# Low parts of every fourth weight block made by an accumulating DMA, in a two-layer decoder trunk in split fp32

## The chip, the cores and the metric

The kernel runs on one core of one Trainium2 chip. The metric is the device time of one launch in microseconds, the median of three runs. The engines are TensorE (PE, with its weight loads PEld), VectorE (DVE), ScalarE (ACT), GpSimd (POOL) and SyncE (SP, which here only issues DMAs).

## The reference

A decoder trunk with D_MODEL = 2048, 256 tokens, two layers, fp32. Layer 0 uses sliding-window attention with sinks, layer 1 block attention with shared keys and values (with 256 tokens it is causal attention over one block). Each layer also has 4 memory heads into 256 memory tokens, one output projection, a layer norm, an MLP with squared ReLU of width 8192, and a second norm:

```python
mix = concat([self_out, mem_out]) @ w_o[layer]
h = layer_norm(ALPHA * h + mix, ln_g[layer, 0], ln_b[layer, 0])
ffn = square(relu(h @ w_up[layer])) @ w_down[layer]
h = layer_norm(ALPHA * h + ffn, ln_g[layer, 1], ln_b[layer, 1])
```

Nearly all the work is matrix products of 256 tokens with some 350 MB of weights, each weight used once.

## The kernel before

Every operand is kept as an exact pair: a high part rounded to the matrix engine's reduced fp32 format (fp32r), and a low part, the rest. A product is then three products of parts: high by high, high by low, low by high. `split()` (L92) makes a pair: ACT rounds (L93), DVE subtracts the high part from the source (L94).

Weights come in blocks of 128 x 2048 (1 MB). `weights()` (L96) asks for a block with one DMA on SP's queue (L102), into one of 4 raw slots (NRAW), and splits it in two halves of 128 x 1024, each into a high and a low tile; there are 7 slots of each (NHI, three and a half blocks). The raw slot is shared with other 1 MB loads: activations and the gain and bias rows of the layer norm. The first three blocks of the kernel come in parts of 4, 2 and 2 (L398 to L400 in `mem_units`), the others in one.

Three routines consume blocks. `wform()` (L137) takes one block for 128 output columns: 16 k-tiles, each with a 512-column product with the high part (L146) and a 256-column one with the low part (L148). `aform()` (L157) takes four blocks, for 512 output columns: 16 k-tiles, each with three 512-column products for either of two token tiles (L168 to L170); `hold` leaves the second token tile's last products for `finish()`. `mem_units()` (L391) does the same as a generator for the memory tokens (L404 to L406).

A layer runs: values (one aform), then four groups of one key and three query blocks and four memory queries (wform), with the attention heads' stages hooked between the products; the output projection (four aforms); the layer norm `normed()` (L343); the MLP in four chunks of 16 wforms (up) and four aforms (down); the second norm. In layer 0 both norms have a filler: the memory products of layer 1 (mem_v, mem_k: four blocks each). In `normed` the transposes of the normed rows stand after units 10, 11, 12 and 16 of the filler (FILL). In layer 1 the first norm has none, and the aform behind it (`wu1`) holds the whole second token tile. The kernel begins with mem_v and mem_k of layer 0.

The framework draws up the order of each engine's instructions when the kernel is built: by program order, where a planner with its own cost estimates holds an operand ready. At run time each engine goes through its own list in that order and waits at each instruction for its operands and its slot. The inverse standard deviation of a norm (`ln_stat`) runs in small steps on POOL (L309 to L313).

Of the kernel before, what the change touches and what calls it, by code (L numbers as in the profile page):

```python
# [17 lines left out]
T = 256  # L18
# [20 lines left out]


class Stages:
    """The heads in flight; each stage of a head runs inside a later block's matrix products."""

    def __init__(self):
        self.heads = []
# [19 lines left out]
WHOOKS = (10, 14, 4)  # L65
NWARM = 2
FILL = (10, 11, 12, 16)
WTAIL = ((1, 2), (2, 0), (3, 1), (5, 2), (7, 1), (9, 2))


@with_exitstack
def trunk(ctx: ExitStack, tc: tile.TileContext, a: dict, out: bass.AP):
# [6 lines left out]
    ps_mm = ctx.enter_context(tc.tile_pool(name="ps_mm", bufs=4, space=PS))  # L79
    ps_at = ctx.enter_context(tc.tile_pool(name="ps_at", bufs=4, space=PS))  # L80

    # ---------------------------------------------------------------- constants
    ident = const.tile([P, P], F32, name="ident")
    make_identity(nc, ident)
    # the tensor engine's clock comes up while the first blocks are on their way
    warm = ap_.tile([P, 512], F32, name="warm", tag="lg", bufs=NLG)
    nc.vector.memset(warm, 0.0)
    ps_warm = ps_at.tile([P, 512], F32, name="ps_warm", tag="at")
    for i in range(NWARM):
        nc.tensor.matmul(ps_warm, warm[:, :P], warm, start=True, stop=True)  # L90
    # ---------------------------------------------------------------- operand splitting
    def split(hi, lo, src):  # L92
        nc.scalar.copy(hi, src)  # L93
        nc.vector.tensor_tensor(lo, src, hi.bitcast(F32), ALU.subtract)  # L94

    def weights(src, parts=1):  # L96
        """One block of weights on chip as exact (hi, lo) pairs, in two halves; the first block
        of all comes in parts, so that the products can begin early."""
        raw = wp.tile([P, 2048], F32, name="raw", tag="raw", bufs=NRAW)
        n = 2048 // parts  # L100
        for c in range(0, 2048, n):
            nc.sync.dma_start(raw[:, c:c + n], src[:, c:c + n])  # L102
        halves = []
        n = min(n, 1024)
        for s in range(2):
            hi = wp.tile([P, 1024], F32R, name="whi", tag="whi", bufs=NHI)
            lo = wp.tile([P, 1024], F32R, name="wlo", tag="wlo", bufs=NHI)
            for c in range(0, 1024, n):
                split(hi[:, c:c + n], lo[:, c:c + n], raw[:, s * 1024 + c:s * 1024 + c + n])
            halves.append((hi, lo))  # L110
        return halves

# [1 line left out]
        return [ap_.tile([P, 4, 2, T], F32R, name=f"{nm}{j}", tag=f"{tag}{j}") for j in range(KT // 4)]  # L114

    def load_act(src, x, j, parts=1):
        """Four k-tiles of an operand on chip as exact (hi, lo) pairs."""
        raw = wp.tile([P, 4, T], F32, name="raw_x", tag="raw", bufs=NRAW)
        n = 4 // parts
        for k in range(0, 4, n):  # L120
            nc.sync.dma_start(raw[:, k:k + n], src[:, 4 * j + k:4 * j + k + n])
            split(x[:, k:k + n, 0], x[:, k:k + n, 1], raw[:, k:k + n])
# [7 lines left out]
                split(xt[2 * j2 + j][:, :, 0, :], xt[2 * j2 + j][:, :, 1, :], raw[:, j])  # L130
        return xt

    # ---------------------------------------------------------------- matrix products
    def nothing():
        pass

    def wform(src, xt, hooks={}):  # L137
        """PSUM [128 columns of W, 512]: xh.W + xl.W as two halves to be added."""
        halves = weights(src)
        ps = ps_mm.tile([P, 2 * T], F32, name="ps_w", tag="mm")  # L140
        for k in range(KT):
            hooks.get(k, nothing)()
            hi, lo = halves[k // 8]
            kk = (k % 8) * P
            x = xt[k // 4][:, k % 4]
            nc.tensor.matmul(ps, hi[:, kk:kk + P], x.rearrange("p s t -> p (s t)"),  # L146
                             start=(k == 0), stop=False)
            nc.tensor.matmul(ps[:, :T], lo[:, kk:kk + P], x[:, 0], start=False, stop=(k == KT - 1))  # L148
        return ps
# [5 lines left out]
        nc.vector.tensor_tensor(dst, ps[:, :T], sb, ALU.add)  # L155

    def aform(srcs, xts, hold=0, hooks={}):  # L157
        """Two PSUM banks [128 tokens, 512 columns] accumulated over 4 k-tiles per block.

        The second token tile's products with the last `hold` k-tiles wait for finish()."""  # L160
        ps = [ps_mm.tile([P, 512], F32, name="ps_a", tag="mm") for _ in range(NT)]
        n = len(srcs)

        def mms(t, k, hi, lo):
            xh = xts[k // 4][:, k % 4, 0, t * P:(t + 1) * P]
            xl = xts[k // 4][:, k % 4, 1, t * P:(t + 1) * P]
            st, en = k == 0, k == 4 * n - 1
            nc.tensor.matmul(ps[t], xh, hi, start=st, stop=False)  # L168
            nc.tensor.matmul(ps[t], xh, lo, start=False, stop=False)  # L169
            nc.tensor.matmul(ps[t], xl, hi, start=False, stop=en)  # L170

        late = []
        for i, src in enumerate(srcs):
            halves = weights(src)
            for q in range(4):
                hi, lo = halves[q // 2]
                c = slice((q % 2) * 512, (q % 2) * 512 + 512)
                args = (4 * i + q, hi[:, c], lo[:, c])
                hooks.get(4 * i + q, nothing)()
                mms(0, *args)  # L180
                if 4 * i + q >= 4 * n - hold:
                    late.append(args)
                else:
                    mms(1, *args)

        def finish():
            for args in late:
                mms(1, *args)

        return ps, finish  # L190

    # ---------------------------------------------------------------- attention
    def evict_v(ps, nm):
        v = ap_.tile([P, NT, 512], F32, name=nm, tag=nm)
        for t in range(NT):
# [1 line left out]
        return v  # L197

    def evict_mk(ps):
        """K of the memory tokens, transposed to [head dim, head, token]; yields before the transposes."""  # L200
        mk = ap_.tile([P, MH, T], F32, name="mk", tag="mk")
        nat = [ap_.tile([P, 512], F32, name="mk_n", tag="lg", bufs=NLG) for _ in range(NT)]
        for t in range(NT):
            nc.scalar.copy(nat[t], ps[t])
        yield mk
        for t in range(NT):
            pt = ps_at.tile([P, 4, P], F32, name="pt_mk", tag="at")
            for m in range(MH):
                nc.tensor.transpose(pt[:, m], nat[t][:, m * P:(m + 1) * P], ident)
            nc.scalar.copy(mk[:, :, t * P:(t + 1) * P], pt)  # L210
        yield

    def head_out(ot, hd, lg, den, spans, v, vcol):
        """Two more stages: probabilities transposed, then O^T as an exact pair."""
        rec = sm.tile([P, NT], F32, name="rec", tag="rec")
        nc.vector.reciprocal(rec, den)
        for t, (c0, n) in enumerate(spans):
# [2 lines left out]
        pt = ps_at.tile([P, 512], F32, name="pt", tag="at")  # L220
        pts = ap_.tile([P, 512], F32, name="pts", tag="pts", bufs=2)
        full = spans[0][1] == T
        # pt columns: [keys 0..127 x all queries | keys 128..255 x later queries]
        dst = 0
        order = [(0, t) for t in range(NT)] + [(1, t) for t in range(NT) if full or t == 1]
        for s, t in order:
# [55 lines left out]
    def new_q():  # L282
        return ap_.tile([P, T], F32, name="qt", tag="qt", bufs=4)

    # ---------------------------------------------------------------- layer norm
    def ln_rows(li, places):
        """gain and bias, each in parts of (pool, tag, bufs, columns), as four pairs of 512 columns."""
        rows = []
        for src, parts in zip((a["ln_g"], a["ln_b"]), places):
            pieces = []  # L290
            for pool, tag, bufs, n in parts:
                r = pool.tile([P, n], F32, name="ln_row", tag=tag, bufs=bufs)
                nc.sync.dma_start(r, bass.AP(tensor=src.tensor, offset=src.offset + li * D + 512 * len(pieces),
                                             ap=[[0, P], [1, n]]))
                pieces += [r[:, c:c + 512] for c in range(0, n, 512)]
            rows.append(pieces)
        return list(zip(*rows))

    def ln_stat(stats):
        """mean and 1/sqrt(var + eps): a bit-level first guess, then Newton's iteration."""  # L300
        mv = sm.tile([P, 2], F32, name="mvar", tag="mvar")
        nc.vector.bn_aggr(mv, stats)
        v = sm.tile([P, 1], F32, name="v", tag="v")
# [16 lines left out]
        nc.vector.scalar_tensor_tensor(ht[:, c], ht[:, c], rstd, b, op0=ALU.mult, op1=ALU.add)  # L320

    def transposed(src, xt, t, j):
        """[128 tokens, 512] -> exact (hi, lo) pair of its transpose, four k-tiles."""
        pt = ps_at.tile([P, 4, P], F32, name="pt_h", tag="at")
        for k in range(4):
            nc.tensor.transpose(pt[:, k], src[:, k * P:(k + 1) * P], ident)  # L326
# [14 lines left out]
        return ap_.tile([P, 4, 2, T], F32R, name=f"{nm}{j}", tag=f"{tag}{j}")  # L341

    def normed(h, st, li, ps, finish, first, filler):  # L343
        """The last residual block, layer norm and the next operand. `filler` holds products that
        need no result of this norm and read the operand's tiles' former contents, block by block."""
        if filler:
            rows = ln_rows(li, [[(wp, "raw", NRAW, D)]] * 2)
        else:
# [38 lines left out]
        nc.vector.scalar_tensor_tensor(u, u, 0.0, u, op0=ALU.max, op1=ALU.mult)  # L387
        split(gt[:, 0], gt[:, 1], u)

    # ---------------------------------------------------------------- the trunk  # L390
    def mem_units(w, xt, out_ps, load=None):  # L391
        """The products of aform(), yielding after each k-tile."""
        ps = [ps_mm.tile([P, 512], F32, name="ps_m", tag="mm") for _ in range(NT)]
        out_ps.extend(ps)
        for i in range(4):
# [28 lines left out]
    for _ in mem_k(0, memt, mem):  # L424
        pass

    # ---------------------------------------------------------------- masks and sinks
    dist_a = const.tile([P, 3 * P], F32, name="dist_a")
    dist_b = const.tile([P, 3 * P], F32, name="dist_b")
    iot = ap_.tile([P, 512], F32, name="iot", tag="lg", bufs=NLG)[:, :3 * P]  # L430
# [133 lines left out]
```

## Time and profile before

| | |
|---|---|
| median of 3 runs | 2058.41 us (2057.87 to 2058.55) |
| profiled execution, span from first to last instruction | 2056.2 us |
| PE busy | 2031.4 us, 10244 matmuls |
| DVE busy | 1229.0 us |
| ACT busy | 916.8 us |
| POOL busy | 28.5 us |
| DMA | 391.73 MB, 191 GB/s mean |

The page gives no time of the profiled execution other than its span; the timed runs lie some 2.2 us above it. A busy PE is not a PE at its peak: matmuls overlap, one of 512 columns is shown as 390 to 400 ns and starts 0.23 us after the one before. A line number is that of the source, and a line in a helper serves all its callers.

### The profile page before, as it was taken

The page shows a single profiled execution, that of the slowest core. Times are in us where ns is not written, and L with a number is a line of the kernel's source. Part 1 is how long each engine was busy: PE and PEld are TensorE (multiplying, and loading weights), DVE is VectorE, ACT ScalarE, POOL GpSimd, SP SyncE. Part 2 cuts the span into 40 slices and gives each one's busy share as a digit, 9 for nine tenths or more (in the row PEclk, how much of TensorE's full clock was granted, in tenths as well). Part 3 has the DMA queues.
Part 4 walks back from the last instruction along what each step waited for, and adds up shares of the span by engine and source line. Part 5 has one row for each costly group of instructions (what it writes and reads, how often), then busy time and mean ns, then how long its engine had stood idle before and what let it go on. Part 6 is the DMA issues. An engine that isn't in the chain of part 4 may idle for free.

```text
span 2056.2 us, 25526 instructions
## 1 busy us (share of the span) xinstructions
PE 2031.4 (99%) x10244; PEld 1721.2 (84%) x10244; DVE 1229.0 (60%) x1621; ACT 916.8 (45%) x1260; POOL 28.5 (1%) x64
## 2 busy tenths in 40 slices
PE   9999999999999999999999999899999999999997
PEld 7888888888888888888888888788888888888886
DVE  6566657655655565566575665675556556555655
ACT  6555534443443444345344554354344434434441
POOL 0000000000000000000010000100000000000001
PEclk9999999999999999999999999999999999999999
DMA  9644546555555555556555446355555555555561
GB/s 348 245 145 154 200 158 246 184 193 196 184 185 199 189 184 189 201 184 226 195 205 178 160 154 210 127 200 189 187 198 188 185 195 188 191 187 192 189 231 62
DMA packets 56279, 391.73 MB, mean 191 GB/s; under 512 B 6368, under 2 KB 6368, under 8 KB 9696
## 3 DMA queue, kind: packets, MB, share of 16 engines
q1 hardware_dynamic: 56160, 390.10, 54.2%
q8 instruction: 80, 1.31, 0.2%
q14 instruction: 39, 0.32, 0.0%
HBM read 387.98 MB, written 2.10 MB: 190 GB/s over the span
## 4 chain that ended last, share of the span: by engine, by line
PE 95%; DVE 3%; POOL 1%; DMA 0%; issue 0%; ACT 0%; SPq 0%; POOLq 0%; DVEq 0%; ACTq 0%
PE ps_w L146 30%; PE ps_w L148 15%; PE ps_a L168 15%; PE ps_a L170 15%; PE ps_a L169 15%; PE ps_m L404 1%; PE ps_m L405 1%; PE ps_m L406 1%; DVE h L320 1%; POOL u L312 1%; DVE wlo L94 1%; PE po L233 1%; PE pt L228 1%; PE ps_s L244 1%; PE pt_h L326 0%
## 5 line engine op out<-in xcount | busy, mean ns | idle before, releaser
L94 DVE TENSOR_TENSOR wlo<-raw,whi 128x1024 fp32r<-128x1024 f32 (+1 forms) x706 | 859.6, 1221 | 736.6 <-ACT whi L93 734.7
L93 ACT CAST whi<-raw 128x1024 fp32r<-128x1024 f32 (+1 forms) x706 | 739.2, 1050 | 998.9 <-PE ps_a L170 527.5
L146 PE MATMUL ps_w<-hT,whi 128*128 128x512 f32 x2304 | 820.2, 400 | 0.5 <-DVE hT L329 0.5
L148 PE MATMUL ps_w<-hT,wlo 128*128 128x256 f32 x2304 | 646.9, 281 | 0.0
L146 PEld LDWEIGHTS ps_w<-hT,whi 128*128 128x128 f32 x2304 | 432.9, 188 | 105.6 <-DVE hT L329 0.8
L148 PEld LDWEIGHTS ps_w<-hT,wlo 128*128 128x128 f32 x2304 | 435.3, 189 | 0.7
L168 PE MATMUL ps_a<-whi,gT 128*128 128x512 f32 x1024 | 398.4, 389 | 0.0
L169 PE MATMUL ps_a<-wlo,gT 128*128 128x512 f32 x1024 | 398.4, 389 | 0.0
L170 PE MATMUL ps_a<-whi,gT 128*128 128x512 f32 x1024 | 398.4, 389 | 0.0
L168 PEld LDWEIGHTS ps_a<-whi,gT 128*128 128x128 f32 x1024 | 192.2, 188 | 40.0
L170 PEld LDWEIGHTS ps_a<-whi,gT 128*128 128x128 f32 x1024 | 192.2, 188 | 39.9
L169 PEld LDWEIGHTS ps_a<-wlo,gT 128*128 128x128 f32 x1024 | 192.2, 188 | 39.7
L146 PE MATMUL ps_w<-xT,whi 128*128 128x512 f32 x320 | 119.9, 414 | 0.0
L168 PE MATMUL ps_a<-whi,ot 128*128 128x512 f32 x256 | 102.1, 399 | 0.0
L169 PE MATMUL ps_a<-wlo,ot 128*128 128x512 f32 x256 | 100.0, 391 | 0.0
L170 PE MATMUL ps_a<-whi,ot 128*128 128x512 f32 x256 | 99.9, 390 | 0.0
L148 PE MATMUL ps_w<-xT,wlo 128*128 128x256 f32 x320 | 89.9, 281 | 0.0
L146 PEld LDWEIGHTS ps_w<-xT,whi 128*128 128x128 f32 x320 | 60.2, 188 | 13.2
L333 DVE SCALAR_TENSOR_TENSOR h<-h,ps_a 128x512 f32<-128x512 f32 x80 | 51.4, 680 | 21.4 <-PE ps_a L170 21.4
L148 PEld LDWEIGHTS ps_w<-xT,wlo 128*128 128x128 f32 x320 | 60.6, 189 | 0.5
L170 PEld LDWEIGHTS ps_a<-whi,ot 128*128 128x128 f32 x256 | 48.2, 188 | 10.1
L168 PEld LDWEIGHTS ps_a<-whi,ot 128*128 128x128 f32 x256 | 48.2, 188 | 9.9
(108 smaller groups left out, 1234.8 us busy)
## 6 DMA issues: line engine op xcount, KB each, us to landing
raw<-in_wdn_dram SPq DMA_DIRECT2D x128, 1024.0 KB, 4.8
raw<-in_wup_dram SPq DMA_DIRECT2D x124, 1024.0 KB, 4.8
raw<-in_wo_dram SPq DMA_DIRECT2D x32, 1024.0 KB, 4.8
raw<-in_wq_dram SPq DMA_DIRECT2D x24, 1024.0 KB, 4.9
raw<-in_wmk_dram SPq DMA_DIRECT2D x8, 1024.0 KB, 6.1
raw<-in_wv_dram SPq DMA_DIRECT2D x8, 1024.0 KB, 6.6
raw<-in_wk_dram SPq DMA_DIRECT2D x8, 1024.0 KB, 4.9
raw<-in_wqm_dram SPq DMA_DIRECT2D x8, 1024.0 KB, 4.8
```

What stands on the lines that cost most here:

```text
L93: nc.scalar.copy(hi, src)
L94: nc.vector.tensor_tensor(lo, src, hi.bitcast(F32), ALU.subtract)
L146: nc.tensor.matmul(ps, hi[:, kk:kk + P], x.rearrange("p s t -> p (s t)"), start=(k == 0), stop=False)
L148: nc.tensor.matmul(ps[:, :T], lo[:, kk:kk + P], x[:, 0], start=False, stop=(k == KT - 1))
L168: nc.tensor.matmul(ps[t], xh, hi, start=st, stop=False)
L169: nc.tensor.matmul(ps[t], xh, lo, start=False, stop=False)
L170: nc.tensor.matmul(ps[t], xl, hi, start=False, stop=en)
L228: nc.tensor.transpose(pt[:, dst:dst + P], lg[:, c0:c0 + P], ident)
L233: nc.tensor.matmul(po[:, :T], v[:, 0, vcol:vcol + P], pts[:, :T], start=True, stop=False)
L244: nc.tensor.matmul(ps[:, P:3 * P], qt[:, P:], kt, start=True, stop=True)
L312: nc.gpsimd.tensor_scalar(u, y, y, w, op0=ALU.mult, op1=ALU.mult)
L333: nc.vector.scalar_tensor_tensor(c, c, ALPHA if first else 1.0, ps[t], op0=ALU.mult, op1=ALU.add)
```

## The change

A counter numbers the blocks that `weights()` makes. In every fourth block (if it comes in one part) the low part is made another way: ACT writes the high part as before, then a second time the same rounding of the source with its sign turned, into the low tile; a DMA issued on GpSimd's queue then adds the raw block's half to it. Raw plus the negated high part is the same low part as before. DVE has no part in these blocks. Docstrings and comments go too.

```diff
+SHARE = 4
...
+    count = [0]
+
     def weights(src, parts=1):
...
         for c in range(0, 2048, n):
             nc.sync.dma_start(raw[:, c:c + n], src[:, c:c + n])
+        count[0] += 1
+        summed = parts == 1 and count[0] % SHARE == 0
         halves = []
         n = min(n, 1024)
         for s in range(2):
             hi = wp.tile([P, 1024], F32R, name="whi", tag="whi", bufs=NHI)
             lo = wp.tile([P, 1024], F32R, name="wlo", tag="wlo", bufs=NHI)
-            for c in range(0, 1024, n):
-                split(hi[:, c:c + n], lo[:, c:c + n], raw[:, s * 1024 + c:s * 1024 + c + n])
+            if summed:
+                src_s = raw[:, s * 1024:(s + 1) * 1024]
+                nc.scalar.copy(hi, src_s)
+                nc.scalar.activation(lo, src_s, AF.Copy, scale=-1.0)
+                nc.gpsimd.dma_start(lo, src_s, accum_op=ALU.add)
+            else:
+                for c in range(0, 1024, n):
+                    split(hi[:, c:c + n], lo[:, c:c + n], raw[:, s * 1024 + c:s * 1024 + c + n])
             halves.append((hi, lo))
```

## Rows read from the trace of the kernel before

**Rows 1.** Page: busy time by engine; chain that ended last, by engine.

```profile
PE 2031.4 (99%) x10244; PEld 1721.2 (84%) x10244; DVE 1229.0 (60%) x1621; ACT 916.8 (45%) x1260; POOL 28.5 (1%) x64
...
PE 95%; DVE 3%; POOL 1%; DMA 0%; issue 0%; ACT 0%; SPq 0%; POOLq 0%; DVEq 0%; ACTq 0%
```

**Rows 2.** Waits of PE: waiter, releaser: us in total, times, longest.

```profile
PE pt_h L326 <- DVE h L320: 5.5, 2, 3.3
PE ps_m L405 <- DVE wlo L94: 2.4, 2, 1.2
...
PE ps_w L146 <- DVE hT L329: 0.5, 1, 0.5
```

**Rows 3.** Page, costliest groups: the two halves of split() for weights.

```profile
L94 DVE TENSOR_TENSOR wlo<-raw,whi 128x1024 fp32r<-128x1024 f32 (+1 forms) x706 | 859.6, 1221 | 736.6 <-ACT whi L93 734.7
L93 ACT CAST whi<-raw 128x1024 fp32r<-128x1024 f32 (+1 forms) x706 | 739.2, 1050 | 998.9 <-PE ps_a L170 527.5
```

**Rows 4.** Timeline, ACT, in a down product: start, duration, idle before.

```profile
820.80 1.06 ACT L93 CAST whi<-raw 128x1024 fp32r<-128x1024 f32 x1 [1.67 <-PE ps_a L170]
823.52 1.05 ACT L93 CAST whi<-raw 128x1024 fp32r<-128x1024 f32 x1 [1.66 <-PE ps_a L170]
...
837.12 1.05 ACT L93 CAST whi<-raw 128x1024 fp32r<-128x1024 f32 x1 [1.67 <-PE ps_a L170]
```

**Rows 5.** Page: load queue (packets, MB, share), and issues with us to landing.

```profile
q1 hardware_dynamic: 56160, 390.10, 54.2%
...
raw<-in_wdn_dram SPq DMA_DIRECT2D x128, 1024.0 KB, 4.8
```

**Rows 6.** DMA view, whole span: the quickest landing of 512 KB.

```profile
ln_row<-in_ln_b_dram SPq DMA_DIRECT2D x1, 512.0 KB, 3.5
```

**Rows 7.** Timeline, ACT and PE, opening: first cast and first low product of block four.

```profile
21.14 2.00 ACT L93 CAST whi<-raw 128x1024 fp32r<-128x1024 f32 x2 [2.54 <-DMA raw<-in_wmv_dram]
...
25.93 0.39 PE L405 MATMUL ps_m<-wlo,memt 128*128 128x512 f32 x1
```

**Rows 8.** DMA view 14 to 52 us; tile raw, 0 to 60 us.

```profile
raw<-in_wmk_dram SPq DMA_DIRECT2D x4, 1024.0 KB, 7.6
...
DMA to landing us min/median/max: 4.8/6.2/10.1
```

**Rows 9.** Windows: stretch, length, busy by engine (count), granted clock, DMA share, GB/s.

```profile
321.00:324.00 3.00, 3.00 (x20) 2.29 (x18) 2.96 (x4) 0.40 (x1) 0.00 (x0) 1.00 0.93 391
1336.00:1342.00 6.00, 5.77 (x20) 4.83 (x21) 5.15 (x9) 1.91 (x4) 0.00 (x0) 0.50 0.00 0
1342.00:1344.00 2.00, 2.00 (x12) 1.64 (x11) 1.92 (x2) 1.48 (x2) 0.00 (x0) 0.99 0.20 29
```

**Rows 10.** Timeline, ACT and PE, first norm of layer 0.

```profile
315.74 2.00 ACT L93 CAST whi<-raw 128x1024 fp32r<-128x1024 f32 x2 [12.00 <-DMA raw<-in_wmv_dram]
318.08 1.07 ACT L328 CAST hT<-pt_h 128x512 fp32r<-128x512 f32 x2 [0.34 <-PE pt_h L326]
...
324.74 0.39 PE L405 MATMUL ps_m<-wlo,memt 128*128 128x512 f32 x1
...
327.49 0.39 PE L405 MATMUL ps_m<-wlo,memt 128*128 128x512 f32 x1
```

**Rows 11.** DMA view, 310 to 330 us.

```profile
raw<-in_wup_dram SPq DMA_DIRECT2D x5, 1024.0 KB, 7.7
```

**Rows 12.** Timeline, ACT and PE, second norm of layer 0.

```profile
1053.09 2.00 ACT L93 CAST whi<-raw 128x1024 fp32r<-128x1024 f32 x2 [11.56 <-DMA raw<-in_wmk_dram]
...
1062.54 0.40 PE L405 MATMUL ps_m<-wlo,memt 128*128 128x512 f32 x1
...
1065.30 0.39 PE L405 MATMUL ps_m<-wlo,memt 128*128 128x512 f32 x1
```

**Rows 13.** DMA view, 1050 to 1068 us.

```profile
raw<-in_wv_dram SPq DMA_DIRECT2D x4, 1024.0 KB, 8.6
```

**Rows 14.** Timeline, ACT and PE, behind the first norm of layer 1.

```profile
1341.85 1.05 ACT L93 CAST whi<-raw 128x1024 fp32r<-128x1024 f32 x1 [1.59 <-PE ps_a L170]
...
1347.55 0.39 PE L169 MATMUL ps_a<-wlo,hT 128*128 128x512 f32 x1
```

**Rows 15.** DMA view, 1338 to 1352 us.

```profile
raw<-in_wup_dram SPq DMA_DIRECT2D x3, 1024.0 KB, 4.9
```

## The prediction

> **What bounds the kernel now.** I read the page's busy shares and its chain first: the matrix engine (PE) is busy 2031.4 us of the 2056.2 us span, and 95% of the chain that ended last is PE; VectorE (DVE) is 3% of it, ScalarE (ACT) 0% [rows 1]. The reader is to see that work taken from DVE shortens nothing by itself; it counts only where PE waited for DVE. The view of who PE waited for says where that was: 5.5 us in two waits of the layer norm's transposes, and 2.4 us in two waits for a low part in the two mem_units fillers [rows 2]. About 8 us is all that a faster DVE could ever give back. The rest of the argument is therefore about lateness: does the low part of every fourth block, which now takes a longer way, still come before PE wants it? That is read from the timelines, stage by stage.
>
> **What the change removes, adds and moves.** There are 352 weight blocks (176 a layer: 4 wv, 4 wk, 12 wq, 4 wqm, 16 wo, 64 up, 64 down, 8 memory), so 88 are summed, and 176 halves. The counter starts with the first memory block and every group is a multiple of four, so a summed block is always the fourth of an aform() or mem_units() call, or every fourth wform(). The first summed one is the fourth block of the kernel: it comes with parts=1.
>
> Removed: 176 DVE subtractions of 1.22 us, 215 us. Added: 176 ACT copies of the shape of the casts at 1.05 us, 185 us [rows 3]. In the steady state neither is seen: ACT casts one half every 2.72 us and has 1.67 us idle before each, until PE gives a slot back [rows 4]; a second 1.05 us fits. Added too: 176 accumulating DMAs of 512 KB on GpSimd's queue, each waiting for ACT's copy. The waits hold GpSimd's own list, where only the layer norm's small Newton steps stand; those come before the filler's fourth block in program order. The raw slot is now given back when the DMA lands, so SP's load of four blocks later waits for it, and the loads behind it on SP's list.
>
> The unknown is X, from the end of ACT's negated copy to the landing of the sum. No row shows an accumulating DMA. Below: a load of 512 KB landed in 3.5 us [rows 6]. Above: the slowest 1 MB load in the busy opening took 10.1 us [rows 8]. I take the 1 MB load of the same stretch, since a sum of 512 KB must fetch 512 KB from each of two places: 4.8 us in the steady state [rows 5], 7.6 in the opening [rows 8], 7.7, 8.6 and 4.9 at the norms [rows 11, 13, 15].
>
> Steady state. With 7 slots, a half's cast starts when PE has done the half seven before, so PE wants the half 6 x 2.72 = 16.3 us after the cast began. Cast and copy take 2.1; the sum has 14.2 us against an X of 4.8, and against 10.1 too. The second limit is the raw slot. Four slots and every fourth block means that a summed block's slot goes to the next summed block: 2.72 + 2.1 until the second half's copy ends, X, and 4.8 for the next load must fit into a block group's 8 x 2.72 = 21.8 us, so X up to 12.1. The load queue has room: 390 MB take 54.2% of the DMA engines' time [rows 5]; 176 sums counted as 1 MB each (185 MB) add 26%. I cost the steady state at nothing; what hides the sum is the 14.2 and 12.1 us, and where a stretch starts with less, it shows. There are four such places.
>
> Opening. The first summed block lands at 21.14, when ACT begins its casts, two in 2.00 us; PE wants the first low half at 25.93 [rows 7]. Cast, copy, cast, copy at that pace: the first copy ends at 23.14, the sum lands 7.6 later at 30.74. PE stands 4.8 us. (The second: 25.14 + 7.6 = 32.74, wanted 2.7 after 30.74; no more.) Then the clock: after the 3.3 us stall of the last norm but one [rows 2] the granted clock was 0.50 (1.2 GHz) from 1336 to 1342, and back by 1342 to 1344 [rows 9]: six microseconds at half speed, 3 us lost. Opening: 4.8 + 3 = 7.8 us, paid once. The following loads have slack again, as PE is later too.
>
> First norm of layer 0. The fourth filler block is cast at 315.74 (two in 2.00); two hT copies of 1.07 together stand ready at 318.08; PE wants the low halves at 324.74 and 327.49 [rows 10]. First copy ends 317.74, plus 7.7 [rows 11] is 325.44: 0.7 late. Second ends 320.8, lands 328.5: 1.0 late, 0.3 of it new. Sum 1.0 us. Second norm: 1053.09 + 2.00 + 8.6 = 1063.7 against 1062.54, and 1053.09 + 4.00 + 1.07 + 8.6 = 1066.8 against 1065.30 [rows 12, 13]: 1.5 us. After stalls of 1.2 us the clock stayed at 1.00 [rows 9], so nothing is added.
>
> First norm of layer 1. The next aform() holds all of its second token tile, so its last half gets a slot only at 1341.85, and PE wants its low part at 1347.55 [rows 14]: 1341.85 + 2.0 + 4.9 [rows 15] = 1348.75, 1.2 late.
>
> Sum: 7.8 + 1.0 + 1.5 + 1.2 = 11.5 us on a span of 2056.2, so 2067.7. The median of the runs, 2058.41, lies 2.2 above that span; with the same 2.2 the forecast is 2069.9. With X at 3.5 everywhere only 0.7 is left (2059.1). With 10.1: opening 7.3 + 3, norms 3.4 + 3, 3.0 + 3 and 6.4 + 3, together 32 (2090.5).
>
> **A rule weighed.** The rows have no sum. The Trainium skill, "DMA: Bandwidth & Descriptors", section "Anatomy of one DMA — SWDGE (gpsimd) path", gives a GpSimd transfer about 2.0 us plus its bytes at 436 GB/s. For 512 KB that is an estimate of 3.2 us: 0.4 us late in the opening and in time elsewhere, 2058.8 in all. What such an X does here stands, from rows, in the first rival below. Against it stands "Collectives: The Full Stack", section "The bandwidth ceiling: the fold count and why AG ≠ RS ≠ AR": an adding transfer runs at half a copy's rate because it reads two sources. No run here shows either yet.
>
> **Rivals.**
> 1. The sums land in time, no change. X near 3.5 even beside loads, or the order drawn up at build time lets PE take the next block's products in the opening. For it: the opening's slack is 25.93 - 23.14 = 2.8 us, and the 512 KB landing misses it by 0.7 only. Against: the stretch's own landings, 7.6 median. Time 2059.1, within 2058 to 2062. Chance 0.25.
> 2. The raw slot's round becomes the bound. From X = 12.1 on, each of the 88 groups grows by the excess. If a sum takes 10.1 and the second half's queues behind the first's, it lands 10.1 + 10.1 - 2.7 = 17.5 after its copy, 5.4 too late: 88 x 5.4 = 475, some 2533 and more. For it: nothing shows how fast DMA engines add, and loads alone keep them 54% busy [rows 5]. Against: 1 MB lands in 4.8. Chance 0.15.
> 3. Faster. DVE loses 2.4 us in each filler norm, where PE waited 1.2 us each time for a low part [rows 2], and DVE does the last norm transposes sooner. If X is under 3, so that the opening keeps its slack, 2.4 us and the 0.5 us of a later wait come back, and up to 5.5 if the layer 1 norm loses a subtraction from its chain: 2058.4 - 8 = 2050 at best. Against: the subtractions that PE waited for belong to blocks one to three, which stay on DVE. It decides at X under 2.8. Chance 0.06.
>
> The forecast keeps 0.54. A measurement tells about 0.2% (4.1 us) from no change: faster 0.05, same 0.26, slower 0.69. The range is 2058 to 2100: it holds the bounds of X in the four places, leaves out rival 2 beyond its beginning (0.13) and most of rival 3 (0.05). The likeliest case's own range is 2063 to 2091.
>
> **What would show it.** Right: PE has a wait of 3 to 7 us for a low part near 26 us with a half-speed stretch behind it, small ones near 325, 1063 and 1348, and none in up and down blocks between 340 and 1000; DVE's subtractions fall from 706 to 530. Wrong: waits of PE for sums that return every four blocks (rival 2), X of 3.5 or less in the opening (rival 1), or a different order of PE's work at the four places, on which all four sums rest.

## The result, and the profile after

The kernel became slower: 2089.98 us as the median of four runs (2088.85 to 2094.6) against 2058.14 for the kernel before beside it. The ratio is 1.0165, with a 95% interval of 1.0153 to 1.0177, or +31.8 us where +11.5 was forecast. The profiled execution took 2088.85 us and its span is 2087.1 us, 30.9 us above that of before.

The page of the changed kernel, with the lines that answer to [rows 1, 3, 5] (busy time; chain by engine; costliest groups; queues with packets, MB and share; issues with KB and median us to landing):

```profile
PE 2038.2 (98%) x10244; PEld 1723.5 (83%) x10244; DVE 1024.2 (49%) x1445; ACT 1084.0 (52%) x1436; POOL 181.7 (9%) x240
...
PE 94%; DMA 3%; DVE 1%; POOL 1%; issue 1%; SPq 0%; ACT 0%; POOLq 0%; DVEq 0%
...
L95 DVE TENSOR_TENSOR wlo<-raw,whi 128x1024 fp32r<-128x1024 f32 (+1 forms) x530 | 645.3, 1220 | 870.3 <-ACT whi L94 870.0
...
L117 ACT ACTIVATE wlo<-raw 128x1024 fp32r<-128x1024 f32 x176 | 186.3, 1060 | 72.3 <-PE ps_a L181 70.6
...
q1 hardware_dynamic: 56160, 390.10, 51.5%
q0 software_dynamic: 25344, 92.29, 22.5%
...
wlo<-raw POOLq DMA_DIRECT2D x176, 512.0 KB, 6.0
```

The work moved as it was meant to: 530 subtractions are left on DVE, ACT makes 176 copies of 1.06 us, 176 sums land in a median of 6.0 us, and the loads in the steady state are nearly as quick as before (`in_wdn`, 128 loads: a median of 5.0 us against 4.8). None of this was on the path. What is new in the chain is the DMA's 3%. Who PE waited for (us in total, times, longest) says where it is, against [rows 2]:

```profile
PE ps_m L417 <- DMA wlo<-raw: 13.7, 3, 5.3
PE ps_a L181 <- DMA wlo<-raw: 6.9, 2, 5.2
PE pt_h L338 <- DVE h L332: 5.6, 2, 3.3
PE ps_m L417 <- DVE wlo L95: 4.5, 3, 2.0
PE ps_m L416 <- ACT whi L94: 3.7, 3, 1.7
```

Five waits for sums cost 20.6 us. With the three lines below them and a constant 1.4 at the start PE's waits are 35.8 us; the same list of the kernel before adds up to 12.0. That is 23.8 us, and PE itself was busy 2038.2 - 2031.4 = 6.8 us longer. Together 30.6 of the 30.9 us.

The chain of waits places them. First the kernel before, then the changed one (start, duration, what; the lines with a matmul or an h are the same work in both):

```profile
61.01 0.87 PE pt_mk L209 x8
...
1077.02 0.87 PE pt_mk L209 x8
...
2033.90 0.70 DVE h L333
```

```profile
24.81 7.77 DMA wlo<-raw
...
68.95 0.87 PE pt_mk L221 x8
...
328.35 13.33 DMA wlo<-raw
...
1073.51 13.01 DMA wlo<-raw
...
1100.32 0.87 PE pt_mk L221 x8
...
1370.66 9.10 DMA wlo<-raw
...
2064.63 0.70 DVE h L345
```

The opening moved everything behind it by 7.94 us; both norms of layer 0 with all that lies between them by 23.30 - 7.94 = 15.36; layer 1's first norm and the held `aform` behind it by the last 30.73 - 23.30 = 7.43. Taken at the same products in the two timelines, the places read: opening 8.0, first norm 7.3, second norm 8.05, behind layer 1's first norm 7.6 (7.4 a few products later), and 0.0 over the whole of layer 0's MLP. The 7.4 is a balance. In the norm itself the changed kernel gains 1.8 us on the one before, because it runs a shorter stretch at half speed there: the granted clock is 1.00 from 1341 to 1346 us and 0.57 from 1360 to 1364, where before it was 0.57 from 1318 to 1322 and 0.50 from 1336 to 1342 [rows 9]. Behind the norm it then loses 9.2.

### The profile page after: what moved, and what is told of

Same layout as the page of the kernel before. It is cut to its first block, busy times and chain, and to the rows that moved or that the text cites. A ratio compares the mean times of both kernels' runs of the same rounds, so it can differ in the third digit from the quotient of the medians.

```text
span 2087.1 us, 26121 instructions
## 1 busy us (share of the span) xinstructions
PE 2038.2 (98%) x10244; PEld 1723.5 (83%) x10244; DVE 1024.2 (49%) x1445; ACT 1084.0 (52%) x1436; POOL 181.7 (9%) x240
## 3 DMA queue, kind: packets, MB, share of 16 engines
q1 hardware_dynamic: 56160, 390.10, 51.5%
q0 software_dynamic: 25344, 92.29, 22.5%
## 4 chain that ended last, share of the span: by engine, by line
PE 94%; DMA 3%; DVE 1%; POOL 1%; issue 1%; SPq 0%; ACT 0%; POOLq 0%; DVEq 0%
PE ps_w L158 29%; PE ps_w L160 15%; PE ps_a L181 15%; PE ps_a L182 15%; PE ps_a L180 15%; DMA wlo<-raw 2%; PE ps_m L417 1%; PE ps_m L418 1%; PE ps_m L416 1%; DMA raw<-in_wmv_dram 1%; PE po L245 1%; PE pt L240 1%; PE ps_s L256 0%; DVE h L332 0%; PE po L247 0%
## 5 line engine op out<-in xcount | busy, mean ns | idle before, releaser
L95 DVE TENSOR_TENSOR wlo<-raw,whi 128x1024 fp32r<-128x1024 f32 (+1 forms) x530 | 645.3, 1220 | 870.3 <-ACT whi L94 870.0
L94 ACT CAST whi<-raw 128x1024 fp32r<-128x1024 f32 (+1 forms) x530 | 554.3, 1048 | 714.3 <-PE ps_a L182 370.8
L118 POOL DMA_DIRECT2D wlo<-raw x176 | 153.3, 871 | 1811.2 <-ACT wlo L117 1375.5
L116 ACT CAST whi<-raw 128x1024 fp32r<-128x1024 f32 x176 | 183.1, 1041 | 84.5 <-PE ps_w L158 52.4
L117 ACT ACTIVATE wlo<-raw 128x1024 fp32r<-128x1024 f32 x176 | 186.3, 1060 | 72.3 <-PE ps_a L181 70.6
L398 DVE TENSOR_TENSOR uu<-ps_w,sb 128x256 f32<-128x256 f32 x124 | 52.0, 420 | 46.6 <-ACT sb L396 46.6
```

The costliest lines, as they stand in the source:

```text
L116: nc.scalar.copy(hi, src_s)
L117: nc.scalar.activation(lo, src_s, AF.Copy, scale=-1.0)
L118: nc.gpsimd.dma_start(lo, src_s, accum_op=ALU.add)
L398: nc.vector.tensor_tensor(u, ps[:, :T], sb, ALU.add)
```

## The experiments

The times to be explained are those four. In each run below the kernel before ran beside it; its median was 2057.55 us for the first four and 2056.54 for the last four. Diffs are against the changed kernel.

**Only the blocks inside the stages.** The five summed blocks at the edges (the fourth of each `mem_units` call and of the held `aform`) go back to DVE.

```diff
-    def weights(src, parts=1):
+    def weights(src, parts=1, edge=False):
...
-        summed = parts == 1 and count[0] % SHARE == 0
+        summed = parts == 1 and count[0] % SHARE == 0 and not edge
...
-            halves = weights(src)
+            halves = weights(src, edge=hold == 16)
...
-            halves = weights(w[i], 1 if load is None else (4, 2, 2, 1)[i])
+            halves = weights(w[i], 1 if load is None else (4, 2, 2, 1)[i], edge=True)
```

> Sums only in the stretches of steady products; the fourth block of the four memory products and of the aform behind layer 1's first norm is subtracted on DVE as before. Theory A (all of the loss is lateness of the sums at the opening, at layer 0's two norms and behind layer 1's first norm): within 3 us of the kernel before, about 2058, with no wait of PE for a sum. Rival B (the sums also cost in the steady state, by ACT's longer list, DMA traffic or the redrawn order): clearly above, 2070 or more.

Measured: 2060.33 us, ratio 1.0014 (1.0005 to 1.0022). Its waits of PE hold none for a sum:

```profile
PE pt_h L338 <- DVE h L332: 5.6, 2, 3.3
PE ps_m L417 <- DVE wlo L95: 4.1, 2, 2.2
```

83 of the 88 blocks are summed here, with 21.5% of the DMA engines' time, and the profiled span is 2056.6 us, 0.4 above before. Inside the stages a sum costs nothing that one profile can show; the medians differ by 2.8 us for all of them together. What this profile does show stands at layer 0's norms and is no sum: the two waits for DVE's low part were 2.4 us in all before [rows 2] and are 4.1 here, and the granted clock behind them is 0.57 (320.5 to 324.5 and 1057.5 to 1061.5 us) where it had been 1.00. The changed kernel has these waits too (2.01 and 1.98 us), but there the sum that lands later decides. Taking 203 us of work off DVE (166 subtractions) gave nothing back either: the 5.6 us of the transposes stand as they did.

**Only the five blocks at the edges.** The same edit with the sign of the condition turned.

```diff
-        summed = parts == 1 and count[0] % SHARE == 0
+        summed = parts == 1 and count[0] % SHARE == 0 and edge
```

> The complement: only the fourth block of the four memory products and of the aform behind layer 1's first norm is summed, 5 blocks of 352. Theory A: nearly the whole loss, 2085 to 2092. Rival B: 2058 to 2072.

Measured: 2086.38 us, ratio 1.0142 (1.0129 to 1.0155), with five waits of PE for sums of 19.6 us together. Five blocks of 88 cost 28.8 us; with the 2.8 of the run before that makes 31.6 of the 31.8. So at this share neither the number of sums nor their load on the DMA engines matters, but the four places do, where these five blocks stand.

**A plain copy in place of the sum.** Same queue, same size, one source, and nothing added.

```diff
-                nc.gpsimd.dma_start(lo, src_s, accum_op=ALU.add)
+                nc.gpsimd.dma_start(lo, hi)
```

> As the changed kernel, but the DMA copies the high part over the low tile instead of adding the raw half, so the low part is not computed; same bytes landed, one source instead of two. If the lateness is that of the add's second source: copies land in about half the time, 6 to 7 us instead of 13 at layer 0's norms, and the time falls to about 2068. If it is the queueing beside the loads and behind the other half: they land within 2 us of the sums, and the time stays within 6 us of 2090.

Measured: 2080.51 us, ratio 1.0117 (1.0102 to 1.0132). Queue and waits of PE:

```profile
q0 software_dynamic: 25344, 92.29, 12.2%
...
PE ps_m L417 <- DMA wlo<-whi: 8.4, 3, 5.7
PE ps_a L181 <- DMA wlo<-whi: 7.2, 3, 6.4
```

176 copies take 12.2% of 2078.4 us, 1.44 us of all 16 DMA engines each; the sums took 22.5% of 2087.1 us, 2.67 each, or 1.85 times as much. Neither expectation was met: the time and the landings lie between the two. The second source decided the outcome at only two of the four places: at the norms of layer 0 the second copy landed after 8.6 and 9.7 us instead of 13.3 and 13.0, and the losses fell from 7.3 and 8.05 to 1.6 and 3.6. In the opening (copy 8.97 us, sum 7.77) and behind layer 1's first norm (8.52, sum 9.10) the loss stayed, at 8.7 and 8.4. There it is the detour over a DMA that costs, not the adding.

**The third block of each four in place of the fourth.**

```diff
-        summed = parts == 1 and count[0] % SHARE == 0
+        summed = parts == 1 and count[0] % SHARE == 3
```

> The third block of every four is summed instead of the fourth (SHARE remainder 3); as many sums less one, in other places: their slots are free and their raw data on chip well before PE wants them at the norms, and in the opening the third block comes in parts and is not summed. Theory A: no late sum at any of the four places, and DVE loses the subtraction that PE waited for at layer 0's norms, so 2053 to 2058. Rival B: still 2070 or more.

Measured: 2063.91 us, ratio 1.0038 (1.0025 to 1.0051); a miss, though most of the loss went. No sum is late at layer 0's norms. In its place PE waits for hT; the wait, and ACT's timeline before the first of the two:

```profile
PE pt_h L338 <- DVE hT L341: 5.4, 2, 2.8
```

```profile
320.98 1.99 ACT L94 CAST whi<-raw 128x1024 fp32r<-128x1024 f32 x2 [3.00 <-PE pt_h L338]
322.88 1.06 ACT L340 CAST hT<-pt_h 128x512 fp32r<-128x512 f32 x2
```

The list drawn up at build puts two casts of a later block ahead of the hT copies that PE wants, and ACT stands 3.00 us before these casts: their block's load, issued at 313.72 us, landed only 7.2 us later. The summed block's place decides that list too, which none of the theories had priced. So block three is a better place for the sum (net 2.6 us at the first norm, 2.9 at the second), but no gain. Behind layer 1's first norm PE does wait for two sums (1.57 and 0.98 us), against the expectation; with the shorter half-speed stretch of that norm the place comes out level (0.3 us gained).

**Every second block, edges left out.** The first experiment with SHARE = 2.

```diff
-SHARE = 4
+SHARE = 2
```

> As e1 (no sums in the memory products and in the held aform), but every second block is summed, twice the sums. Loads hold the DMA engines 52% of the time and a sum 2.67 us of all 16, so about 95% in all. If the steady state hides the sums by its 12 to 14 us (theory A), and the traffic still fits: within 10 us of e1, 2058 to 2070, with a sum landing 8 to 10 us after issue. If the raw slot's round is already near its end in e1 (the rival of the prediction): waits of PE every two blocks, 2150 or more.

Measured: 2098.59 us, ratio 1.0204 (1.019 to 1.0218); neither time was met, though the sums landed after 9.1 us in the median, as theory A had it. A window over the up and down products of layer 0 but their end (stretch, length, busy by engine, granted clock, DMA share, GB/s), and the longest wait of PE, at that end:

```profile
385.00:997.00 612.00, 603.04 (x3062) 511.29 (x3061) 219.90 (x312) 365.16 (x447) 95.52 (x110) 1.00 1.00 282
```

```profile
995.94 0.79 PE L181 MATMUL ps_a<-wlo,gT 128*128 128x512 f32 x1 [8.10 <-DMA wlo<-raw]
```

The DMA engines are full (share 1.00) for 612 us, and still PE loses only 0.9 us until the end of the stretch; then 8.1 us are lost in one wait. PE's waits for sums are 17.4 us in the whole run. The other losses lie at layer 0's norms, where PE waits 11.2 us for DVE's low parts, and in layer 0's heads, where it waits 4.7 us for copies of ACT and DVE. So a limit begins in the steady state at this share of sums: loads and sums together take 93.7% of the engines' time, against 74.0% with every fourth block. Whether it is the full engines or the round of the raw slot that rival 2 feared (a sum here took up to 14.4 us, and the round had room for 12.1) is not shown. What bunches the transfers at 980 to 990 us was not traced further.

**The first half of the summed block alone, and the second half alone.** The other half goes to DVE. The pair asks why the second sum of a block is the late one: whether it queues behind the first, or shares the engines with the loads released beside it.

```diff
-            if summed:
+            if summed and s == 0:
```

> The changed kernel, but in a summed block only the first half is summed; the second half is subtracted on DVE. In the changed kernel the first sum at layer 0's norms landed 5.6 to 5.9 us after its issue and the second 13.0 to 13.3. Theory C (the second sum is late because it shares the DMA engines with three loads issued beside it, behind the first): the norms lose at most 2 us each and the held aform 2 to 3, the opening keeps its 8: 2066 to 2074. Rival D (any sum at these places is late, by ACT's two passes or GpSimd's issue): 2080 or more.

Measured: 2070.98 us, ratio 1.0071 (1.0058 to 1.0085), the time that theory C expected. The sums at the four places landed after 8.3, 5.6, 5.6 and 4.6 us, and the places lost 7.8, 3.9, 0.0 and 1.5. The 3.9 at the first norm are more than expected and no sum's: PE waits 2.8 us there for hT.

```diff
-            if summed:
+            if summed and s == 1:
```

> The complement: only the second half of a summed block is summed. Theory C: the norms keep most of their loss (4 to 8 us each), the sum landing 9 to 13 us after its issue though nothing of its own queue is ahead of it; the opening loses less than 8 because PE wants the second half later: 2073 to 2086. Rival D: as the first half alone, within 3 us of it.

Measured: 2073.79 us, ratio 1.0081 (1.0067 to 1.0095). The time is within theory C's range, but it also lies within 3 us of the first half alone (2.8), so the landings have to decide, and they are theory C's. No other sum stands in the queue here, and still, in the chain of waits:

```profile
322.45 12.06 DMA wlo<-raw
...
1065.62 11.77 DMA wlo<-raw
```

With nothing of its own kind ahead, the second half's sum takes 12.06 and 11.77 us: queueing behind the first half explains 1.3 us at most of the 13.3 and 13.0. The first half alone takes 5.6; it was issued 2.3 us after its block's first cast, the second half alone 3.3. What changes in between is the loads. At the norms, when the fillers' last blocks are cast, raw slots come back and SP asks for three megabytes within 2 us. The DMA view of the changed kernel, for what is issued between 328 and 329 us:

```profile
raw<-in_wup_dram SPq DMA_DIRECT2D x1, 1024.0 KB, 12.8
wlo<-raw POOLq DMA_DIRECT2D x1, 512.0 KB, 13.3
```

A sum of half a megabyte, issued at 328.35, and a load of one megabyte, issued at 328.67, land within 0.2 us of each other (341.68 and 341.48). The sum gets through no sooner than the load beside it. The same view for 331.5 to 334.5 us, and then for 334.5 to 340, says where its time goes (q0 holds the sums, q1 the loads; packets, MB, share of the 16 engines):

```profile
q1 hardware_dynamic: 120, 0.97, 98.9%
q0 software_dynamic: 6, 0.00, 0.2%
...
q1 hardware_dynamic: 171, 1.16, 53.8%
q0 software_dynamic: 141, 0.52, 47.4%
```

For three microseconds the engines move a load that was asked for at 327.54, before the sum, and next to nothing of the sum; then the sum and the next load have about half of them each. With the second half alone it is the same, though the load was asked for at 322.75 us, while GpSimd was still issuing the sum (322.45 to 323.37): from 323 to 327.5 us only q1 moves (0.97 MB), from 327.5 to 332.5 q0 has 51.6% and q1 51.1%. With the first half alone the sum was asked for at 325.47, 1.05 us before the next load, and it went first: from 326.5 to 330 us only q0 moves (0.51 MB).

The two halves cost 14.4 and 17.3 us, which happens to make 31.7; place by place they do not add up (opening 7.8 and 4.1, where both together cost 8.0; first norm 3.9 and 5.2 against 7.3).

**One block in all: the second of the held `aform`.** Where PE waits 3.3 us in layer 1's first norm, three subtractions stand in DVE's chain. Could one summed block take them out?

```diff
-    def weights(src, parts=1):
+    def weights(src, parts=1, early=False):
...
-        summed = parts == 1 and count[0] % SHARE == 0
+        summed = early
...
-            halves = weights(src)
+            halves = weights(src, early=hold == 16 and i == 1)
```

> One block in all is summed: the second of the aform behind layer 1's first norm, whose two subtractions stand on DVE inside the norm's second chain (1.1 us each). Its casts come 14 us before PE wants the low parts, while the DMA engines are idle. If DVE's list is what sets that chain, PE's 3.3 us wait there shrinks by up to 2.3 us and the half-speed stretch behind it by up to as much: 2053 to 2056. If GpSimd's issue of the sums delays the norm's Newton steps on the same list, that is taken back: 2057 to 2060.

Measured: 2062.63 us, ratio 1.0029 (1.0019 to 1.0039); a miss. ACT's and GpSimd's timelines:

```profile
1313.31 1.04 ACT L116 CAST whi<-raw 128x1024 fp32r<-128x1024 f32 x1 [0.30 <-PE ps_a L182]
...
1322.99 2.01 ACT L117 ACTIVATE wlo<-raw 128x1024 fp32r<-128x1024 f32 x2
```

```profile
1324.37 1.95 POOL L118 DMA_DIRECT2D wlo<-raw  x2 [9.74 <-ACT wlo L117]
```

The casts end at 1314.35, but the list has the negated copies behind hT copies and other casts, so that the sums leave at 1324.37 and land 5.5 and 10.3 us later; PE waits 3.6 and 3.1 us for them. One of the two waits for the transposes is gone (2.2 us of 5.5 are left) and two larger ones have come.

No version tried beats the kernel before. Holding back the three loads at the norms of layer 0 until the sum has landed was not tried.

## Why the prediction was right and wrong, step by step

**What bounds the kernel: right.** PE is 94% of the chain after, and 205 us less on DVE (1229.0 to 1024.2) gave nothing back.

**Steady state at nothing: right.** Between 345 and 1056 us PE waits for nothing, and the first experiment shows the same with 83 blocks. The two limits that the prediction worked out, 14.2 us until PE wants the half and 12.1 for the raw slot's round, stand above what was measured: 6.0 in the median of all sums, and 11.0 at most in layer 0's MLP. The sums' share was forecast at 26% and is 22.5%.

**Opening: the sum right, two of its terms off against each other.** Forecast 7.8, measured 8.0. X was taken at 7.6, and the sum landed 7.77 after its issue, 8.1 after the end of the copy. But the raw block itself came later: its casts began at 22.48, not 21.14. In the traces of all versions this start lies between 20.66 and 22.70, and what moves it stays open. So PE stood longer than the 4.8 of the forecast, first 1.70 us for the high part of a later block that its list puts here, then 4.52 for the sum. And the half speed behind it cost 1.7 us where the forecast had 3 (below). That 7.8 and 8.0 agree so well is luck. The timeline of PE in the changed kernel at the four places (start, duration, idle before):

```profile
27.37 0.73 PE L416 MATMUL ps_m<-whi,memt 128*128 128x512 f32 x2 [1.70 <-ACT whi L94]
32.62 0.79 PE L417 MATMUL ps_m<-wlo,memt 128*128 128x512 f32 x1 [4.52 <-DMA wlo<-raw]
...
328.70 0.50 PE L417 MATMUL ps_m<-wlo,memt 128*128 128x512 f32 x1 [2.01 <-DVE wlo L95]
...
341.73 0.50 PE L417 MATMUL ps_m<-wlo,memt 128*128 128x512 f32 x1 [3.88 <-DMA wlo<-raw]
...
1086.56 0.79 PE L417 MATMUL ps_m<-wlo,memt 128*128 128x512 f32 x1 [5.32 <-DMA wlo<-raw]
...
1372.77 0.50 PE L181 MATMUL ps_a<-wlo,hT 128*128 128x512 f32 x1 [1.71 <-DMA wlo<-raw]
...
1379.81 0.80 PE L181 MATMUL ps_a<-wlo,hT 128*128 128x512 f32 x1 [5.16 <-DMA wlo<-raw]
```

**X at the three norms: the step that failed.** The prediction took "7.7, 8.6 and 4.9 at the norms" from the median landing of the loads there [rows 11, 13, 15], one value for both halves of a block. The first halves came sooner (5.6, 5.9 and 5.0 us from their issue), and it is the second halves that PE waits for: 13.3, 13.0 and 9.1 us. At the first norm the prediction's own sum with 13.3 in place of 7.7 gives 1.0 + 5.6 = 6.6 late, where it had 1.0; measured 7.3, the clock's part in it. At the second it gives 1.5 + 4.4 = 5.9, and 8.05 was measured with 2.0 of clock. The way of reckoning, landing against the moment at which PE wants it, was right, and the size of X was wrong: a median over a stretch hides the one moment at which three loads leave together, and that is just when the second half's sum leaves. With its bound of 10.1 the forecast gave 6.4 and 6.0 for these two norms, still too little; that bound came to 32 us in all because it overpriced the other two places (10.3 and 9.4).

Why 13 and not 8 at layer 0's norms is shown from three sides: a plain copy in the sum's place takes 8.6 and 9.7, the second sum without the first takes 12.06 and 11.77, and the DMA views show the sum standing behind one load and then sharing the engines with the next. So it is an adding transfer among three loads, and its place behind the first sum on GpSimd's queue is worth 1.3 us at most.

Behind layer 1's first norm X is only half of the miss. The prediction let each copy follow its cast at once (1341.85 + 2.0). ACT's timeline of the changed kernel, and GpSimd's, show another order:

```profile
1363.23 1.05 ACT L116 CAST whi<-raw 128x1024 fp32r<-128x1024 f32 x1 [1.59 <-PE ps_a L182]
1364.96 1.05 ACT L94 CAST whi<-raw 128x1024 fp32r<-128x1024 f32 x1 [0.69 <-PE ps_a L182]
1365.92 0.58 ACT L340 CAST hT<-pt_h 128x512 fp32r<-128x512 f32 x1
1366.39 2.01 ACT L117 ACTIVATE wlo<-raw 128x1024 fp32r<-128x1024 f32 x2
```

```profile
1367.75 0.92 POOL L118 DMA_DIRECT2D wlo<-raw  x1 [10.16 <-ACT wlo L117]
1370.66 0.87 POOL L118 DMA_DIRECT2D wlo<-raw  x1 [1.99 <-ACT whi L94]
```

The copies stand behind the next block's cast and an hT copy, and end at 1368.40; the second sum leaves only at 1370.66, by the profile after yet another cast. Counted from the second half's cast, the landing at 1379.76 comes 16.5 us later, where the forecast had 2.0 + 4.9 = 6.9: 5.4 of the 9.6 us between them lie before the issue (7.4 from cast to issue against 2.0), some 3 of them by the list's order and 2.3 between the copy's end and the issue; 4.2 are the transfer. Here the single wait of 1.2 us became two of 1.71 and 5.16. In the run with the second half alone that sum landed after 4.5 us and PE waited 1.2, just as forecast. With both halves, the issue at 1370.66 came 0.04 us behind that of a load, and the DMA view shows the load going first: from 1371.7 to 1375.5 us the loads' queue has 93.1% of the engines and the sums' 0.5%, from 1375.5 to 1379.5 the sums' 66.2% and the loads' 9.7%. Why GpSimd issued it only 2.3 us after the copy's end stays open.

**No clock loss at the norms: failed with it.** The prediction had waits of 1.2 us there and read from [rows 9] that the clock holds through them. The waits before the stretches below were 2.0 to 5.3 us. Windows of the changed kernel, with columns as in [rows 9]:

```profile
29.00:36.00 7.00, 3.38 (x8) 2.70 (x9) 4.13 (x4) 2.20 (x3) 0.00 (x0) 0.51 0.98 266
329.00:333.00 4.00, 4.00 (x16) 3.38 (x15) 1.51 (x3) 0.00 (x1) 0.22 (x1) 0.57 0.99 229
...
1084.00:1091.00 7.00, 4.44 (x11) 3.53 (x12) 4.06 (x6) 4.57 (x6) 0.00 (x0) 0.52 0.96 350
...
1378.00:1384.00 6.00, 4.19 (x10) 3.33 (x11) 0.69 (x1) 0.60 (x1) 0.00 (x0) 0.50 0.62 202
```

Behind the waits the granted clock is 0.50 to 0.57 of full speed (0.57 from 343 to 347 us too), that is at half speed (1.2 GHz) for most of these windows. Products that lie 0.23 us apart at full speed lie 0.43 apart there: eight of them behind 32.62, five from 343.23, ten behind 1086.56 and ten behind 1379.81, together about 1.7 + 1.0 + 2.0 + 2.2 = 6.9 us. That this is so near the 6.8 us by which PE's busy time grew is chance: the stretch from 329 to 333 us costs some 1.6 more (an estimate from the same spacings), and layer 1's first norm gives 1.8 back. The 3 us that the prediction took for one such stretch were too many, and none at the norms too few.

**The rivals.** The first (sums in time) fell at the first block: the slack of 2.8 us stood against 7.77. Its other way, PE taking the next block's products first, came about for two products only, and then PE waited. The second (a return every four blocks) did not come; the fifth experiment, with twice the sums, has thirteen waits for sums, far from one in every group. The third would have needed an X under 2.8, and the quickest sum landed after 4.4 us. The estimate of 3.2 us from the Trainium skill, "DMA: Bandwidth & Descriptors", section "Anatomy of one DMA — SWDGE (gpsimd) path", is thus below every sum of this kernel; the measurement decides. The rule weighed against it, "Collectives: The Full Stack", section "The bandwidth ceiling: the fold count and why AG ≠ RS ≠ AR", says that the adding step of a collective runs at half the rate of its copying step, because it reads two sources. That is said of transfers between cores; the sums inside one core agree with it: 1.85 times a copy's engine time.

## What to carry to other kernels

Price an added transfer by what is released at the same moment as it, not by the median landing of its stretch, and price the last one of a group: here that was 13 us against 7.7, because a load asked for at nearly the same time went first. A detour that hides well inside a stage (83 of 88 blocks) can lose everything at the few places where slack is short, so list these first and leave them out of the change, or choose another block there. And look at what the framework's list does with the moved work: three times here a copy or cast that was cheap in itself stood ahead of what was urgent, and cost several microseconds.

## What the runs showed of the hardware that was not expected

- A 512 KB accumulating DMA takes 2.67 us of all 16 DMA engines, a 512 KB copy inside the chip 1.44, and a 1 MB load 2.89 (51.5% of 2087.1 us for the 372 loads of 1 MB that 390.10 MB make). Half a megabyte added costs the engines nearly as much as a whole one loaded.
- A sum issued beside a load of twice its size landed with it, 13.3 and 12.8 us after their issues, though each was on its own queue. A load asked for 0.8 us before the sum had the engines first (98.9% of them for 3 us); a sum asked for 1.05 us before the next load went ahead of that load and took 5.6 us.
- DMA engines that were busy all of 612 us (share 1.00) kept PE fed with a loss of 0.9 us until the end of that stretch, where one wait of 8.1 us came.
- One wait of 2.0 us for a low part (328.70 us) was enough here to be followed by a granted clock of 0.57 in the next window; [rows 9] had shown waits of 1.2 us without one. It is not the wait's length alone: behind one of 2.3 us (1341.51 us, in layer 1's first norm) the clock stayed at 1.00.
